# Dilated attention in a hybrid decoder layer: a step takes four heads in the first group and eight in the other two

## The chip, the core and the metric

The kernel runs on one core of a Trainium2 chip. The core has a matrix engine (PE in the profile; its weight loads are a row of their own, PEld), a vector engine (DVE), a scalar engine (ACT), GpSimd (POOL) and SyncE (SP), which here issues most of the loads. Each engine works through its own list of instructions in order and waits for the others at semaphores. The metric is the device time of one launch in microseconds (us); lower is better.

## The reference, cut to what matters

One decoder layer over 512 tokens of 1024 features: an input projection, two token mixers side by side (retention, and a dilated attention), a gated merge, an MLP and a last gated residual. The part that matters here is the dilated attention: 24 heads of 64 features in three groups of eight, with dilations 1, 4 and 16.

```python
DIL_GROUPS = ((128, 1), (512, 4), (2048, 16))      # (window, dilation)
s  = einsum('bcnqhe,bcnkhe->bcnhqk', qs, kk) * hd ** -0.5     # scores, per head
s  = where(mask, s, -1e30)
lse = logsumexp(s, axis=-1)
pr  = exp(s - lse[..., None])
o   = einsum('bcnhqk,bcnkhe->bcnqhe', pr, vv)
...
w = softmax(stack(lses), axis=0)                   # the three groups are merged by their denominators
out = sum(w[..., None] * stack(outs), axis=0)
```

With 512 tokens, each group has four blocks of 128 queries. In group 0 a block sees its own 128 keys and, from the second block on, the 128 before them, so its scores are 128 columns wide in the first block and 256 in the other three. In groups 1 and 2 a block sees 128 keys.

## The kernel before

The layer is one long program of matmuls on PE. Large projections (`gemm`, line 239) keep PE busy; every fp32 operand of theirs is split into a high and a low part (`split`, line 71: ACT writes the high part, DVE the difference), and a product is three matmuls (`PASSES`). The weights come in through SP as tiles of 512 KB (`load_next`, line 94), are split into one of five `w` tiles (`prep_next`, line 109) and are consumed by the matmuls of line 234, each with 512 columns, 24 for one output tile of 128 rows in a projection of depth 1024.

The dilated attention runs inside this stream. `attention` (line 453) makes a list of steps, and `filler` (line 215) hands that list to `pump` (line 205), which is called after every third matmul of a projection and takes out steps at a rate that spreads the whole list over 84 such calls. A unit of attention is one block of 128 queries with `n` heads, and it has three steps:

- `scores` (line 468): one matmul per head (line 475) on 64 partitions of the query and key tiles, the even head on partitions 0 to 63 and the odd one on 64 to 127, into two PSUM banks, `sb[0]` for even heads and `sb[1]` for odd ones. Then DVE adds the mask and takes the row maximum (line 479, per head), scales the maxima (line 482, once), and ACT takes the exponential (line 484, per head, through the helper at line 66).
- `flip` (line 487): PE transposes the exponentials, one 128x128 block at a time (line 493), into a PSUM bank, and ACT copies the bank to SBUF (line 495).
- `weigh` (line 497): two rows of PE work per block of 128 keys and head, with 64 columns each (line 505), sum the values into a bank that belongs to the block of queries; the bank is copied out when all eight heads are in it (line 510).

The steps of three units are staggered: weigh of unit i-2, flip of unit i-1, scores of unit i. A unit has two heads in group 0 and four in groups 1 and 2, so the lists are 48, 24 and 24 steps long.

What stands in which order on an engine is decided by a scheduler when the program is built; the list of steps gives it the program order, and it moves an instruction back when its inputs or its buffer would not be there in time. So transposes and score matmuls of neighbouring steps may end up mixed on PE.

Two pools of SBUF tiles matter: `t` (`big`, 4 KB per partition, 25 tiles), which also holds the weight tiles on their way in, and `s` (`half`, 2 KB, 12 tiles). The PSUM pool of `bank` has four banks.

Of the kernel before, what the change touches and what calls it, by code (L numbers as in the profile page):

```python
# [16 lines left out]
S, D, P = 512, 1024, 128  # L17
# [7 lines left out]
MAGIC = 12582912.0  # L25
TWO_PI = (6.25, 17 / 512, -37 / 2 ** 21, 2 * math.pi - (6.25 + 17 / 512 - 37 / 2 ** 21))
PI_IN = 3.1415925
N_RAW, N_W, N_T, N_S = 4, 5, 25, 12


@with_exitstack
def hybrid_block(ctx, tc, a, out):
    nc = tc.nc
# [12 lines left out]
    def nm(s):  # L46
        count[0] += 1
        return f"{s}{count[0]}"

    def big(shape=(P, D), dtype=F32):  # L50
        return pt.tile(list(shape), dtype, name=nm("t"), tag="t")

    def half(shape=(P, 512), dtype=F32):
        return psm.tile(list(shape), dtype, name=nm("s"), tag="s")

    def stat(n=1):
        return pst.tile([P, n], F32, name=nm("st"), tag=f"st{n}")

    def bank():
        return pps.tile([P, 512], F32, name=nm("b"), tag="ps")  # L60
# [4 lines left out]
    def act(o, i, f=AF.Copy, **kw):  # L65
        nc.scalar.activation(o, i, f, **kw)  # L66
# [39 lines left out]
    def new_w():  # L106
        return pw.tile([P, 2, 2, 512], F32R, name=nm("w"), tag="w")
# [161 lines left out]
    ident = const.tile([P, P], F32, name="ident")  # L269
# [58 lines left out]
    for i in range(4):  # L328
        w = new_w()
        r = pop()  # L330
        for j in range(2):
            f = 2 * i + j
            g = cols[:, 0, f:f + 1]
# [54 lines left out]
    def pair_tiles():  # L388
        return [big((P, 2, 512)) for _ in range(2)]

    def at(pair, i):
        return pair[i // 2][:, i % 2, :]
# [60 lines left out]
    def attention(g, qT, kT, v):  # L453
        n_g = pair_tiles()
        N.append(n_g)
        pairs = 1 if g == 0 else 2
        pvs = {}

        def unit(t, p0):
            nb = 2 if g == 0 and t > 0 else 1  # L460
            w = nb * P
            k0 = (t - nb + 1) * P
            s0, n = 2 * p0, 2 * pairs
            mk = masks[:, 2 - nb:2, :].rearrange("p a b -> p (a b)") if g == 0 else masks[:, g, :]
            mv, dv = M[g][:, t, s0:s0 + n], DEN[g][:, t, s0:s0 + n]
            got = {}

            def scores():
                sb = [bank(), bank()]
                sm = got["p"] = half((P, n, w))  # L470
                st = stat(4)
                for i in range(n):
                    q, hh = divmod(i, 2)
                    rows = slice(hh * 64, hh * 64 + 64)
                    nc.tensor.matmul(sb[hh][:, q * w:(q + 1) * w], at(qT, p0 + q)[rows, t * P:(t + 1) * P],  # L475
                                     at(kT, p0 + q)[rows, k0:k0 + w], start=True, stop=True)
                for i in range(n):
                    q, hh = divmod(i, 2)
                    nc.vector.tensor_tensor_reduce(  # L479
                        out=sm[:, i, :], in0=sb[hh][:, q * w:(q + 1) * w], in1=mk, scale=1.0, scalar=NEG,  # L480
                        op0=OP.add, op1=OP.max, accum_out=mv[:, i:i + 1])
                nc.vector.tensor_scalar(st[:, :n], mv, -0.125, None, op0=OP.mult)  # L482
                for i in range(n):
                    act(sm[:, i, :], sm[:, i, :], AF.Exp, bias=st[:, i:i + 1], scale=0.125,
                        accum_out=dv[:, i:i + 1])

            def flip():
                sm = got["p"]
                tb = bank()
                for i in range(n):  # L490
                    for j in range(nb):
                        c = i * nb + j
                        nc.tensor.transpose(tb[:, c * P:(c + 1) * P], sm[:, i, j * P:(j + 1) * P], ident)  # L493
                pT = got["t"] = half()
                act(pT[:, :n * w], tb[:, :n * w])

            def weigh():
                if t not in pvs:
                    pvs[t] = [bank(), 0]
                pv = pvs[t][0]  # L500
                for i in range(n):
                    s = s0 + i
                    for j in range(nb):
                        c = i * nb + j
                        nc.tensor.matmul(pv[:, s * HD:(s + 1) * HD], got["t"][:, c * P:(c + 1) * P],  # L505
                                         at(v, t - nb + 1 + j)[:, s * HD:(s + 1) * HD],
                                         start=(j == 0), stop=(j == nb - 1))
                pvs[t][1] += n
                if pvs[t][1] == NS:
                    nc.vector.tensor_copy(at(n_g, t), pv)  # L510

            return scores, flip, weigh

        us = [unit(t, p0) for t in range(NT) for p0 in range(0, 4, pairs)]
        steps = []
        for i in range(len(us) + 2):
            for lag in (2, 1, 0):
                if 0 <= i - lag < len(us):
                    steps.append(us[i - lag][lag])
        return steps  # L520
# [7 lines left out]
    for g in range(NG):  # L528
        vs, qT, kT = pair_tiles(), pair_tiles(), pair_tiles()
        gemm(4, uT, plain_evac(vs), k_outer=(g == 0))  # L530
        if g == 0:
            nc.vector.tensor_copy(posr, posr_i)
            rotary(0)

            def tables():
                row_tables()
                scale_rotary(0)
            later(4, tables)
            vc = vs
        else:  # L540
            vc = pair_tiles()
            stream_order(lambda c: at(vc, c), lambda t: at(vs, t))
        gemm(4, uT, rope_evac(qT, g > 0), wstat=True)
        gemm(4, uT, rope_evac(kT, g > 0), wstat=True)
        if g == 0:
            rotary(1)
            scale_rotary(1)
        filler(attention(g, qT, kT, vc), 84, 10)
        if g == 1:
            stream_order(lambda c: sc[0][:, c], lambda t: M[0][:, t])  # L550
            stream_order(lambda c: sc[1][:, c], lambda t: DEN[0][:, t])
# [349 lines left out]
    pT = []  # L901
# [207 lines left out]
    for t in range(NT):  # L1109
        parts_n = 1 if t < NT - 1 else 2  # L1110
        w = 512 // parts_n
# [88 lines left out]
```

## Time and profile before

| | |
|---|---|
| median of 3 runs | 1226.34 us (1225.99 to 1228.89) |
| profiled execution | 1226.16 us, of which the profile's span is 1224.3 us |
| PE busy | 1210.2 us (99%), 5646 matmul rows |
| DVE, ACT, POOL busy | 803.5 us (66%), 595.0 us (49%), 61.5 us (5%) |
| DMA | 158.86 MB, mean 130 GB/s |
| chain that ended last | PE 94%; of it line 234 52%, line 475 2%, line 505 2%, line 493 1% |

PE is busy in nearly every slice of the span. That does not say that it streams at full rate: the profile counts a matmul as busy from its start to its modelled end, and neighbours overlap, so what a piece of PE work costs is read from the starts of the rows around it. A score matmul of line 475 and a weighing matmul of line 505 stand as two rows each in the trace, a transpose of line 493 and a matmul of line 234 as one.

### The profile page before, as it was taken

The page shows a single profiled execution, that of the slowest core. Times are in us where ns is not written, and L with a number is a line of the kernel's source. Part 1 is how long each engine was busy: PE and PEld are TensorE (multiplying, and loading weights), DVE is VectorE, ACT ScalarE, POOL GpSimd, SP SyncE. Part 2 cuts the span into 40 slices and gives each one's busy share as a digit, 9 for nine tenths or more (in the row PEclk, how much of TensorE's full clock was granted, in tenths as well). Part 3 has the DMA queues.
Part 4 walks back from the last instruction along what each step waited for, and adds up shares of the span by engine and source line. Part 5 has one row for each costly group of instructions (what it writes and reads, how often), then busy time and mean ns, then how long its engine had stood idle before and what let it go on. Part 6 is the DMA issues. An engine that isn't in the chain of part 4 may idle for free.

```text
span 1224.3 us, 15136 instructions
## 1 busy us (share of the span) xinstructions
PE 1210.2 (99%) x5646; PEld 990.9 (81%) x5646; DVE 803.5 (66%) x1215; ACT 595.0 (49%) x991; POOL 61.5 (5%) x112
## 2 busy tenths in 40 slices
PE   9999999999999999999999999999999999999996
PEld 7877777887788888888888888887888888888885
DVE  6743643563366895968859555773585776875696
ACT  7344444437765563544535642355544553543362
POOL 1002001000000000000000011020000000000210
PEclk9999999999999999999999999999999999999998
DMA  9422132262105354232435454827132341255401
GB/s 338 152 104 71 60 95 88 69 214 88 44 22 194 137 181 155 85 114 96 145 121 185 134 209 143 297 82 275 52 129 77 121 175 66 86 172 172 155 18 69
DMA packets 53321, 158.86 MB, mean 130 GB/s; under 512 B 8832, under 2 KB 9088, under 8 KB 53248
## 3 DMA queue, kind: packets, MB, share of 16 engines
q1 hardware_dynamic: 39552, 131.82, 30.9%
q10 hardware_dynamic: 9600, 14.53, 3.7%
q0 software_dynamic: 4096, 11.55, 2.6%
q8 instruction: 44, 0.72, 0.2%
q14 instruction: 29, 0.24, 0.1%
HBM read 139.47 MB, written 14.68 MB: 126 GB/s over the span
## 4 chain that ended last, share of the span: by engine, by line
PE 94%; DVE 2%; DMA 1%; ACT 1%; issue 1%; POOL 0%; SPq 0%; DVEq 0%; POOLq 0%; ACTq 0%
PE a L234 52%; PE b L705 15%; PE a L1029 11%; PE a L705 7%; PE b L475 2%; PE b L792 2%; PE b L505 2%; PE b L493 1%; PE b L777 1%; DMA t<-in_w_in_dram 1%; DVE t L294 1%; PE b L813 1%; DVE w L69 0%; DVE s L69 0%; DVE t L69 0%
## 5 line engine op out<-in xcount | busy, mean ns | idle before, releaser
L69 DVE TENSOR_TENSOR w<-t,w 128x1024 fp32r<-128x1024 f32 (+1 forms) x248 | 296.0, 1202 | 152.8 <-ACT w L66 148.4
L66 ACT ACTIVATE w<-t 128x1024 fp32r<-128x1024 f32 (+1 forms) x248 | 257.7, 1045 | 266.5 <-PE a L234 91.3
L234 PE MATMUL a<-u,w 128*128 128x512 f32 x1536 | 374.5, 397 | 0.0
L234 PEld LDWEIGHTS a<-u,w 128*128 128x128 f32 x1536 | 282.3, 188 | 62.1 <-issue 4.0
L69 DVE TENSOR_TENSOR t<-t,t 128x1024 f32<-128x1024 f32 (+4 forms) x179 | 184.8, 1056 | 21.0 <-ACT t L66 18.9
L705 PE MATMUL b<-w,t 128*128 128x512 f32 x696 | 162.5, 389 | 0.0
L705 PEld LDWEIGHTS b<-w,t 128*128 128x128 f32 x696 | 130.6, 188 | 27.1
L1029 PE MATMUL a<-u,w 128*128 128x512 f32 x576 | 134.0, 389 | 0.0
L1029 PEld LDWEIGHTS a<-u,w 128*128 128x128 f32 x576 | 108.1, 188 | 22.5
L234 PE MATMUL a<-w,u 128*128 128x512 f32 (+1 forms) x504 | 116.7, 385 | 1.2 <-ACT w L66 1.0
L234 PE MATMUL a<-t,w 128*128 128x512 f32 x480 | 110.5, 390 | 0.0
L234 PEld LDWEIGHTS a<-w,u 128*128 128x128 f32 x504 | 90.2, 189 | 19.5 <-ACT w L66 1.4
L234 PEld LDWEIGHTS a<-t,w 128*128 128x128 f32 x480 | 89.7, 188 | 18.9 <-DVE t L69 0.3
L234 PE MATMUL a<-w,t 128*128 128x512 f32 x432 | 99.7, 390 | 0.0
L234 PEld LDWEIGHTS a<-w,t 128*128 128x128 f32 x432 | 80.7, 188 | 16.7
L69 DVE TENSOR_TENSOR t<-a,t 128x512 f32<-128x512 f32 x72 | 55.5, 773 | 54.6 <-ACT t L66 31.3
L66 ACT ACTIVATE s<-b 128x512 f32<-128x512 f32 (+1 forms) x74 | 44.7, 606 | 88.7 <-PE b L493 36.0
L479 DVE CUSTOM_DVE_ANT_0 s<-b,masks 128x128 f32<-128x128 f32 (+1 forms) x96 | 27.2, 319 | 83.3 <-PE b L475 83.2
L66 ACT ACTIVATE t<-t 128x512 fp32r<-128x512 f32 (+1 forms) x55 | 42.1, 788 | 38.6 <-DVE t L69 38.5
L66 ACT ACTIVATE s<-s,st 128x128 f32<-128x128 f32 (+1 forms) x96 | 40.0, 418 | 26.5 <-DVE st L482 26.4
L66 ACT ACTIVATE t<-s 128x256 f32<-128x256 f32 (+3 forms) x94 | 41.7, 488 | 22.1 <-DVE s L69 20.3
L66 ACT ACTIVATE s<-a 128x512 f32<-128x512 f32 x56 | 32.7, 593 | 38.7 <-PE a L234 30.3
(119 smaller groups left out, 1018.7 us busy)
## 6 DMA issues: line engine op xcount, KB each, us to landing
t<-in_w_in_dram SPq DMA_DIRECT2D x104, 512.0 KB
t<-in_w_down_dram SPq DMA_DIRECT2D x38, 512.0 KB
t<-in_w_up_dram SPq DMA_DIRECT2D x32, 512.0 KB
t<-in_w_ret_out_dram SPq DMA_DIRECT2D x16, 512.0 KB
t<-in_x_dram SPq DMA_DIRECT2D x8, 512.0 KB
yrd<-s ACTq DMA_DIRECT2D x16, 256.0 KB
t<-yrd SPq DMA_DIRECT2D x16, 256.0 KB
t<-in_w_o_dram SPq DMA_DIRECT2D x8, 512.0 KB
```

Of the source, the lines that this page charges most:

```text
L66: nc.scalar.activation(o, i, f, **kw)
L69: nc.vector.tensor_tensor(o, x, y, op=op)
L234: nc.tensor.matmul(ps, l, r, start=(k == 0 and q == 0), stop=(k == n - 1 and q == 2))
L294: return nc.vector.scalar_tensor_tensor(o, x, s, y, op0=op0, op1=op1)
L475: nc.tensor.matmul(sb[hh][:, q * w:(q + 1) * w], at(qT, p0 + q)[rows, t * P:(t + 1) * P], at(kT, p0 + q)[rows, k0:k0 + w], start=True, sto ...
L479: nc.vector.tensor_tensor_reduce(out=sm[:, i, :], in0=sb[hh][:, q * w:(q + 1) * w], in1=mk, scale=1.0, scalar=NEG, op0=OP.add, op1=OP.max, ...
L493: nc.tensor.transpose(tb[:, c * P:(c + 1) * P], sm[:, i, j * P:(j + 1) * P], ident)
L505: nc.tensor.matmul(pv[:, s * HD:(s + 1) * HD], got["t"][:, c * P:(c + 1) * P], at(v, t - nb + 1 + j)[:, s * HD:(s + 1) * HD], start=(j == ...
L705: nc.tensor.matmul(ps[t], f(k, i, t), w[:, j, k2], start=(first and k == 0 and n == 0), stop=(k == 3 and n == 2), skip_group_check=not first)
L777: nc.tensor.matmul(b[:, :w], kT[d][:, i1, j * P:(j + 1) * P], qT[d][:, i2, j * P:], start=(n == 0), stop=(n == 5))
L792: nc.tensor.matmul(b, sc[j][:, i1, c:c + P], vh[j][:, i2, :], start=(n == 0), stop=(n == last))
L1029: nc.tensor.matmul(state["ps"][t], w[:, i, k2, t * P:(t + 1) * P], vT[:, x, k], start=(k == 0 and n == 0), stop=(k == 7 and n == 2))
```

## The change

`pairs`, the number of head pairs in a unit, goes from 1 to 2 in group 0 and from 2 to 4 in groups 1 and 2. A unit then has four or eight heads, and the lists of steps are 24, 12 and 12 long. What a unit needs grows with it: the score tile and the transposed tile become `big` tiles, the vector of scaled maxima has eight columns, and `flip` fills two banks one after the other, with a copy behind each. The pools go to 26 `t` tiles and 10 `s` tiles. Nothing else is edited; line numbers behind line 497 move by one, the transposes to line 495, their copies to 496 and the weighing matmuls to 506.

```diff
-N_RAW, N_W, N_T, N_S = 4, 5, 25, 12
+N_RAW, N_W, N_T, N_S = 4, 5, 26, 10
...
-        pairs = 1 if g == 0 else 2
+        pairs = 2 if g == 0 else 4
...
                 sb = [bank(), bank()]
-                sm = got["p"] = half((P, n, w))
-                st = stat(4)
+                sm = got["p"] = big((P, n, w))
+                st = stat(8)
...
             def flip():
                 sm = got["p"]
-                tb = bank()
-                for i in range(n):
-                    for j in range(nb):
-                        c = i * nb + j
-                        nc.tensor.transpose(tb[:, c * P:(c + 1) * P], sm[:, i, j * P:(j + 1) * P], ident)
-                pT = got["t"] = half()
-                act(pT[:, :n * w], tb[:, :n * w])
+                pT = got["t"] = big((P, n * w))
+                for h0 in range(0, n * w, 512):
+                    tb = bank()
+                    m = min(512, n * w - h0)
+                    for c in range(h0 // P, (h0 + m) // P):
+                        i, j = divmod(c, nb)
+                        nc.tensor.transpose(tb[:, c * P - h0:(c + 1) * P - h0], sm[:, i, j * P:(j + 1) * P], ident)
+                    act(pT[:, h0:h0 + m], tb[:, :m])
```

The built programs differ in their order from the first score matmul to the end of the attention; ahead of it and behind it the engines' instructions stand in the same order. Three places on PE follow. In the rows, `a` is an accumulator of a projection, `b` a bank, and a row ends with the size of what it writes and with how often it is repeated.

Group 0, last block of queries, before: the scores of a unit (line 475, 256 columns) between the transposes (line 493) of the unit ahead of it.

```order
L234 MATMUL a_1273<-u_134,w_1154 128x512 x3
L493 MATMUL b_1263<-ident,s_1236 128x128 x2
L475 MATMUL b_1280<-t_254,t_252 128x256
L493 MATMUL b_1263<-ident,s_1236 128x128 x2
L475 MATMUL b_1281<-t_254,t_252 128x256
L234 MATMUL a_1273<-u_134,w_1154 128x512 x3
```

The same block of queries now: four heads, with the two even ones and the two odd ones in a stretch each.

```order
L234 MATMUL a_1229<-u_134,w_883 128x512 x6
L475 MATMUL b_1236<-t_254,t_252 128x256 x2
L234 MATMUL a_1229<-u_134,w_1103 128x512 x5
L475 MATMUL b_1237<-t_254,t_252 128x256 x2
L234 MATMUL a_1229<-u_134,w_1103 128x512
```

The transposes have left this place, and two heads on the same partitions follow each other.

Group 2, last block of queries, before: four heads (line 475), each on its own between transposes.

```order
L234 MATMUL a_2686<-u_134,w_2577 128x512 x2
L493 MATMUL b_2671<-ident,s_2616 128x128
L475 MATMUL b_2693<-t_1518,t_1516 128x128
L493 MATMUL b_2671<-ident,s_2616 128x128
L475 MATMUL b_2694<-t_1518,t_1516 128x128
L493 MATMUL b_2671<-ident,s_2616 128x128
L475 MATMUL b_2693<-t_1518,t_1516 128x128
L493 MATMUL b_2671<-ident,s_2616 128x128
L475 MATMUL b_2694<-t_1518,t_1516 128x128
L234 MATMUL a_2686<-u_134,w_2577 128x512 x4
```

The same block now: all eight heads in one stretch, even and odd in turn.

```order
L234 MATMUL a_2587<-u_134,w_2307 128x512 x5
L475 MATMUL b_2594<-t_1466,t_1464 128x128
L475 MATMUL b_2595<-t_1466,t_1464 128x128
L475 MATMUL b_2594<-t_1466,t_1464 128x128
L475 MATMUL b_2595<-t_1466,t_1464 128x128
L475 MATMUL b_2594<-t_1467,t_1465 128x128
L475 MATMUL b_2595<-t_1467,t_1465 128x128
L475 MATMUL b_2594<-t_1467,t_1465 128x128
L475 MATMUL b_2595<-t_1467,t_1465 128x128
L234 MATMUL a_2587<-u_134,w_2491 128x512 x6
```

Four stretches of one head have become one of eight.

Group 1, first block of queries, before: the four heads of the first unit, and the first transpose of that unit behind 17 matmuls of the projection.

```order
L475 MATMUL b_1567<-t_708,t_706 128x128
L475 MATMUL b_1568<-t_708,t_706 128x128
L475 MATMUL b_1567<-t_708,t_706 128x128
L475 MATMUL b_1568<-t_708,t_706 128x128
L234 MATMUL a_1548<-w_1453,u_134 128x512 x6
L234 MATMUL a_1591<-w_1199,u_134 128x512 x6
L234 MATMUL a_1591<-w_1420,u_134 128x512 x5
L493 MATMUL b_1598<-ident,s_1569 128x128
```

The same place now: the second four of eight heads, and the first transposes (line 495) behind 19 matmuls.

```order
L475 MATMUL b_1529<-t_709,t_707 128x128
L475 MATMUL b_1530<-t_709,t_707 128x128
L475 MATMUL b_1529<-t_709,t_707 128x128
L475 MATMUL b_1530<-t_709,t_707 128x128
L234 MATMUL a_1522<-w_1362,u_134 128x512 x4
L234 MATMUL a_1522<-w_1386,u_134 128x512 x6
L234 MATMUL a_1522<-w_1397,u_134 128x512 x6
L234 MATMUL a_1577<-w_1166,u_134 128x512 x3
L495 MATMUL b_1582<-ident,t_1531 128x128 x4
```

Between the scores and the transposes DVE and ACT now have eight heads to treat in place of four, and PE has nearly as much other work there as before.

## Rows read from the trace of the kernel before

**Rows 1.** Head of the profile's page, and its row of the projections' weight loads.

```profile
span 1224.3 us, 15136 instructions
L234 PEld LDWEIGHTS a<-u,w 128*128 128x128 f32 x1536 | 282.3, 188 | 62.1 <-issue 4.0
```

**Rows 2.** Windows: the attention stretch; stretch, length, busy us of each engine (instructions), clock.

```profile
81.73:350.37 268.64, 268.05 (x1378) 209.66 (x1378) 129.14 (x320) 138.79 (x312) 17.27 (x32) 1.00 0.26 83
```

**Rows 3.** Chain of waits, behind the attention stretch; start us, length us, what.

```profile
...
349.90 0.67 PE b L505 x6
...
373.12 0.44 PE b L588 x4
...
384.83 35.38 PE a L234 x156
```

**Rows 4.** Timeline of PE, group 0, first token tile; start us, length us, what.

```profile
89.85 0.86 PE L234 MATMUL a<-w,u 128*128 128x512 f32 x3
90.64 0.49 PE L475 MATMUL b<-t,t 64*128 64x128 f32 x4
91.06 1.66 PE L234 MATMUL a<-w,u 128*128 128x512 f32 x6
92.56 0.22 PE L505 MATMUL b<-t,s 128*128 128x64 f32 x1
```

**Rows 5.** Timeline of PE, group 1.

```profile
211.68 1.54 PE L234 MATMUL a<-u,w 128*128 128x512 f32 x6
213.15 0.71 PE L475 MATMUL b<-t,t 64*128 64x128 f32 x8
213.80 3.02 PE L234 MATMUL a<-u,w 128*128 128x512 f32 x12
216.66 0.33 PE L505 MATMUL b<-t,s 128*128 128x64 f32 x2
```

**Rows 6.** Timeline of PE, group 0, a later token tile (256 columns).

```profile
117.73 0.40 PE L234 MATMUL a<-u,w 128*128 128x512 f32 x1
118.06 0.70 PE L475 MATMUL b<-t,t 64*128 64x256 f32 x4
118.69 1.64 PE L234 MATMUL a<-u,w 128*128 128x512 f32 x6
120.17 0.44 PE L505 MATMUL b<-t,s 128*128 128x64 f32 x3
```

**Rows 7.** Timeline of PE, group 0, scores and transposes mixed.

```profile
130.58 1.32 PE L234 MATMUL a<-u,w 128*128 128x512 f32 x5
131.74 0.38 PE L493 MATMUL b<-ident,s 128*128 128x128 f32 x2
132.05 0.70 PE L475 MATMUL b<-t,t 64*128 64x256 f32 x2
...
133.67 0.96 PE L234 MATMUL a<-u,w 128*128 128x512 f32 x3
134.47 0.33 PE L505 MATMUL b<-t,s 128*128 128x64 f32 x2
```

**Rows 8.** Timeline of PE, group 2, scores and transposes mixed.

```profile
327.44 1.98 PE L234 MATMUL a<-u,w 128*128 128x512 f32 x8
...
331.89 2.56 PE L234 MATMUL a<-u,w 128*128 128x512 f32 x10
334.30 0.33 PE L505 MATMUL b<-t,s 128*128 128x64 f32 x2
```

**Rows 9.** Groups by form: busy us, mean ns of one, idle before and releaser.

```profile
L66 ACT ACT_TABLE_LOAD x25 | 32.1, 1283 | 5.9 <-DMA t<-t 2.8 <-ACT s L66 1.6 <-PEq L1189 1.2
...
L66 ACT ACTIVATE s<-s,st 128x128 f32<-128x128 f32 x72 | 28.1, 391 | 18.4 <-DVE st L482 18.3
...
L479 DVE CUSTOM_DVE_ANT_0 s<-b,masks 128x128 f32<-128x128 f32 x72 | 17.5, 285 | 60.4 <-PE b L475 60.4
```

**Rows 10.** The page's row of the weights' first copies, with ScalarE's idle time before them.

```profile
L66 ACT ACTIVATE w<-t 128x1024 fp32r<-128x1024 f32 (+1 forms) x248 | 257.7, 1045 | 266.5 <-PE a L234 91.3
```

## The prediction

> **What bounds the kernel now.** I read the views from the outside in. The head of the page gives a span of 1224.3 us [rows 1]; the profiled execution took 1226.16 us, and the sum below is made against that. The windows of the attention stretch, from the first score matmul to the last weighing one, show PE busy for 268.05 of 268.64 us at the full granted clock, 2.4 GHz, while DVE is busy for 129 and ACT for 139 [rows 2]. So only what PE itself does, or is made to wait for, counts here. The chain of waits gives PE's undisturbed rates behind the stretch: 156 projection matmuls in 35.38 us, 0.227 us each; four transposes in 0.44 us, 0.11 each; six weighing rows in 0.67 us, 0.112 each [rows 3].
>
> With these rates the stretch can be taken apart. Of its 1378 PE rows [rows 2], 96 heads of two rows are scores, 120 transposes and 240 weighing rows, which leaves 826 projection matmuls: 826 x 0.227 = 187.5 us, 120 x 0.11 = 13.2, 240 x 0.112 = 26.9. The scores are left with 268.6 - 227.6 = 41.0 us, 0.43 us a head, though a head's matmul writes only 128 or 256 columns. The timeline of PE shows why. I price a stretch of scores from the start of a projection row ahead of it to the start of the row behind the next projection matmuls, less 0.227 for each of those:
>
> - two heads of 128 columns: 92.56 - 89.85 = 2.71, less nine matmuls: 0.67 us [rows 4];
> - four heads of 128 columns: 216.66 - 211.68 = 4.98, less 18 matmuls: 0.89 us [rows 5].
>
> Two further heads add 0.22, so a head costs 0.11 and a stretch, whatever its length, 0.45: what PE pays to go over to matmuls on 64 partitions and back. Two heads of 256 columns: 120.17 - 117.73 = 2.44, less seven matmuls, 0.85 [rows 6], so 0.20 a head beside the 0.45. Where transposes stand between the scores, every piece pays again: two single heads of 256 columns between four transposes take 134.47 - 130.58 = 3.89, less eight matmuls (1.82) and four transposes (0.44): 1.63, or 0.82 a piece [rows 7]; four single heads of 128 columns take 334.30 - 327.44 = 6.86, less 18 matmuls (4.09) and four transposes (0.44): 2.33, or 0.58 a piece [rows 8].
>
> **The change part by part.** *Scores on PE.* Their matmuls are the same 96; what changes is into how many stretches the order cuts them. In the order before there are 52: of 128 columns fifteen with one head, five with two, one with three, eleven with four; of 256 columns sixteen with one, four with two. In the order after there are 24: of 128 columns two with one, one with two, five with four, six with eight; of 256 columns two with one, two with three, two with four, and four in which two heads on the same partitions follow each other.
>
> Before: 15 x 0.58 + 5 x 0.67 + 0.89 (three heads priced as four) + 11 x 0.89 = 22.7, and 16 x 0.82 + 4 x 0.85 = 16.5; together 39.2 us. The 1.8 us to the 41.0 left above are short waits and other seams.
>
> After: eight heads of 128 columns are not in the trace. Bounds: one stretch of four, 0.89, below, and two such stretches, 1.78, above; I take 0.45 + 8 x 0.11 = 1.33, since the rows with two and four heads differ by just this slope. Four of 256 columns likewise: 0.45 + 4 x 0.20 = 1.25 (between 0.85 and 1.70), three the same 1.25. Two heads on the same partitions can't run side by side: between a pair, 0.85, and two single pieces, 1.63, I take the middle, 1.24. Sum: 2 x 0.58 + 0.67 + 5 x 0.89 + 6 x 1.33 = 14.3, and 2 x 0.82 + 2 x 1.25 + 2 x 1.25 + 4 x 1.24 = 11.6; together 25.9 us. Saved: 39.2 - 25.9 = 13.3 us.
>
> *Transposes and weighing.* Their counts stay 120 and 120. They run on all 128 partitions like the projections, and a transpose costs the same 0.11 alone or in eights as far as rows 3 tell, so I cost the grouping at nothing.
>
> *DVE and ACT.* Sixteen scalings of maxima and two bank copies go, and the order has 15 table loads of ACT where the trace shows 25, at 1.28 us each [rows 9]. All this is covered by PE, which pauses for 0.6 us in the whole stretch [rows 2]; it is worth nothing on the path, and if a wait for ACT should appear these 12.8 us only help.
>
> *Longer steps.* In a unit the work of DVE and ACT between scores and transposes doubles. A reduction keeps DVE busy for 17.5/72 = 0.24 us and an exponential ACT for 28.1/72 = 0.39 [rows 9], so eight heads need 8 x 0.24 + 8 x 0.39 = 5.0 us until the last exponential, but the first transpose needs only the first: 1.9 + 0.4 = 2.3. In the order PE has 19 projection matmuls (4.3 us) between them in the first unit of group 1, 20 in that of group 2, and about 50 (11.4 us) in the others of these groups. There each transpose of the second bank comes one matmul after the other, 0.34 us apart, about the pace of the exponentials. I cost the waits at nothing here and carry them as a rival.
>
> *Tiles.* Scores and transposed scores now live in the pool that also takes the weight loads, which grows by one tile. ACT's first copy of a weight tile waits, by its releaser, for PE to free a split tile, not for a load [rows 10], so loads are early, and I cost this at nothing.
>
> The sum: 1226.16 - 13.3 = 1212.9 us. The median of the runs shown is 0.18 above the profiled execution, hence 1213.0.
>
> **The rivals.** *The exponentials come late.* Eight heads need 5.0 us and the shortest distance is 4.3: 0.7 us short at the two first units, more if ACT has weight copies of 1.05 us [rows 10] in between. If each of the 16 units lost 0.45 us, 7.2 in all, the time would be 1220.2. For it speaks that one more bank than the pool of four is asked for in a step; against it, that 14 units have more room, and that PE lost only 0.6 us of the whole stretch before [rows 2], where 17 matmuls lay at the place of these 19.
>
> *Only pairing pays.* If a stretch had no price of its own and just a head without a partner on the other 64 partitions were dear, the gain would be that of the pairs alone: a single head costs 0.82 - 0.65 = 0.17 more at 256 columns and 0.58 - 0.56 = 0.02 at 128, so 16 x 0.17 + 15 x 0.02 = 3.0 before, and 12 x 0.17 + 2 x 0.02 = 2.1 after; 0.9 us saved, 1225.3. Against it: rows 4 and 5 are both fully paired, and the second pair costs a third of the first. A rule of the Trainium skill leads to this rival: "TensorE: Matmul & The Clock Gate", Part 3 on packing small matmuls, says that a weight load overlaps with running matmuls only when its row group differs. By it every projection matmul would show its load, and going over to the scores would cost nothing special. The trace disagrees: loads of 0.188 us [rows 1] on the same 128 rows lie behind each other's matmuls at 0.227 a step [rows 3].
>
> *Weights come late, and the kernel is slower.* Up to two score tiles and two transposed ones now hold `t` tiles, three more than the pool grew by, and a weight load must wait until PE has weighed a unit before it finds a tile. Place: the split of the next projection's weights, and PE's line 234 behind it. The stretch holds 826/96 = 8.6 projections; the gain is eaten from 13.3/8.6 = 1.5 us of wait in each, and at 2.1 us the time is 1231. Against it stands rows 10: ACT waits there for PE.
>
> **How the numbers follow.** The forecast's own range: if the unexplained 1.8 us go too, and the same-partition pairs cost 0.85, 13.3 + 1.8 + 1.6 = 16.7 are saved, 1209.6 by the median; rounding of 52 prices by 0.02 adds 1.0, hence 1208.6. If eight heads cost 1.78 and those pairs 1.63, 13.3 - 2.7 - 1.6 = 9.0, hence 1217.3. Late exponentials reach to 1220.2, and I let the range end there. Chances: forecast 0.82, late exponentials 0.10, only pairing 0.03, late weights 0.03, and 0.02 for more gain than the range holds. A measurement of this kernel tells about 0.3%, 3.7 us, from no change. Faster by more than that: 0.82 + 0.09 + 0.02 = 0.93; within it: 0.01 of the late exponentials and only pairing, 0.04; slower: 0.03.
>
> **What would show it.** In the timeline after, a stretch of eight score heads (16 rows of line 475) should cost 1.33 us by the same reckoning; 1.78 or more says that the price goes with the heads. The stretch of attention should be some 13 us shorter for nearly the same number of projection matmuls, with PE busy throughout. Waits of PE at line 495 for ACT would show late exponentials, waits of line 234 for ACT or DVE with a DMA ahead late weights. The prediction is wrong if the attention stretch keeps its length, or if the gain is there and lost again behind it.

## The result and the profile after

The changed kernel takes 1212.24 us (median; 1212.09 to 1212.70) beside 1226.26 us for the kernel before in the same session: a ratio of 0.9882, with a 95% interval of 0.9868 to 0.9895. That is 14.0 us less; the prediction was 1213.0 us, 13.3 less than the median it started from.

The head of the page, and three of its groups (columns as in [rows 9]):

```profile
span 1210.6 us, 15131 instructions
...
L66 ACT ACTIVATE w<-t 128x1024 fp32r<-128x1024 f32 (+1 forms) x248 | 256.9, 1044 | 261.9 <-PE a L234 93.7
...
L234 PE MATMUL a<-u,w 128*128 128x512 f32 x1536 | 369.0, 395 | 1.0 <-ACT t L66 1.0
L234 PEld LDWEIGHTS a<-u,w 128*128 128x128 f32 x1536 | 284.0, 188 | 62.1 <-issue 2.3
```

The span is 13.7 us shorter. The weight copies of ScalarE have the same duration and releaser as in [rows 10]. The chain of waits of this trace can be followed back only to 64 us before the end, so the stages are read from the windows: ahead of the first score matmul, from there to the last weighing one, and behind it (columns as in [rows 2]).

```profile
0.00:83.20 83.20, 80.47 (x344) 65.61 (x344) 52.83 (x78) 40.97 (x64) 4.78 (x12) 1.00 0.62 218
83.20:336.25 253.05, 252.83 (x1372) 206.46 (x1371) 129.54 (x318) 129.26 (x306) 17.27 (x32) 1.00 0.27 88
336.25:1210.60 874.35, 863.58 (x3934) 717.25 (x3932) 618.42 (x804) 408.83 (x609) 39.46 (x68) 1.00 0.38 135
```

The attention stretch went from 268.64 us [rows 2] to 253.05, 15.6 less. It starts 1.5 us later and holds six PE rows fewer (1372, not 1378): six projection matmuls, 1.4 us, now stand ahead of it. The rest, 14.2 us, is gained inside the stretch; what lies behind is 0.4 us longer (873.93 us before). The granted clock is full in all three.

By the prediction's reckoning, 820 projection matmuls take 186.1 us, 120 transposes 13.2 and 240 weighing rows 26.9, so that the scores are left with 26.8 us, where they had 41.0.

Timeline of PE, group 2: a stretch of eight heads (start us, length us, what).

```profile
312.82 3.57 PE L234 MATMUL a<-u,w 128*128 128x512 f32 x15
316.32 1.16 PE L475 MATMUL b<-t,t 64*128 64x128 f32 x16
317.41 5.06 PE L234 MATMUL a<-u,w 128*128 128x512 f32 x21
322.31 1.89 PE L506 MATMUL b<-t,t 128*128 128x64 f32 x16
```

322.31 - 312.82 = 9.49, less 36 projection matmuls (8.17): 1.32 us for eight heads, where four cost 0.89 [rows 5].

The same view in group 0: twice two heads of 256 columns on the same 64 partitions. At two other places of this group the even and odd heads of a unit stand together, eight rows of 256 columns; one of them comes second.

```profile
144.60 1.29 PE L234 MATMUL a<-u,w 128*128 128x512 f32 x5
145.82 1.13 PE L475 MATMUL b<-t,t 64*128 64x256 f32 x4
146.88 1.43 PE L234 MATMUL a<-u,w 128*128 128x512 f32 x5
148.24 1.13 PE L475 MATMUL b<-t,t 64*128 64x256 f32 x4
149.30 1.19 PE L234 MATMUL a<-u,w 128*128 128x512 f32 x4
150.32 0.33 PE L506 MATMUL b<-t,t 128*128 128x64 f32 x2
```

```profile
99.91 1.13 PE L475 MATMUL b<-t,t 64*128 64x256 f32 x8
100.97 2.33 PE L234 MATMUL a<-u,w 128*128 128x512 f32 x9
```

The first gives (150.32 - 144.60 - 14 x 0.227) / 2 = 1.27 us for two heads. From the first score row to the next projection row it is 1.06 us in both fences: four heads in pairs cost what two heads on one half cost.

What going over to 64 partitions does is seen most directly in the waits of the weight loads (engine, line, what ended the wait: us in total, times, longest), before and then after, in the attention stretch.

```profile
PEld b L475 <- issue: 10.0, 38, 0.4
PEld a L234 <- issue: 4.0, 12, 0.3
PEld b L493 <- ACT s L66: 2.2, 5, 1.0
```

```profile
PEld b L475 <- issue: 6.3, 20, 0.4
PEld a L234 <- issue: 2.3, 7, 0.3
PEld b L495 <- ACT t L66: 0.9, 3, 0.3
```

"Issue" means that nothing in the profile ended the wait: the load of the first score of a stretch stood still though its inputs were there, 38 times before and 20 times after, for 0.26 and 0.32 us on average. The second line is the way back, the first load of a projection behind the scores: 12 times and 7. The last line is where late exponentials would stand: 0.9 us after, less than the 2.2 us before.

ScalarE and VectorE, the lines that answer to [rows 9]:

```profile
L66 ACT ACTIVATE t<-t,st 128x128 f32<-128x128 f32 x72 | 27.9, 390 | 14.5 <-DVE st L482 14.5
L66 ACT ACT_TABLE_LOAD x15 | 19.2, 1283 | 4.0 <-DMA t<-t 1.9 <-PEq L1190 1.2 <-ACT s L66 0.8
...
L479 DVE CUSTOM_DVE_ANT_0 t<-b,masks 128x128 f32<-128x128 f32 x72 | 16.2, 285 | 16.7 <-PE b L475 16.7
```

The ten table loads did go.

### The profile page after: what moved, and what is told of

Its sections match the earlier page's. It is cut to its first block, busy times and chain, and to the rows that moved or that the text cites. A ratio compares the mean times of both kernels' runs of the same rounds, so it can differ in the third digit from the quotient of the medians.

```text
span 1210.6 us, 15131 instructions
## 1 busy us (share of the span) xinstructions
PE 1196.9 (99%) x5646; PEld 989.3 (82%) x5646; DVE 800.8 (66%) x1199; ACT 579.1 (48%) x979; POOL 61.5 (5%) x112
## 5 line engine op out<-in xcount | busy, mean ns | idle before, releaser
L234 PE MATMUL a<-u,w 128*128 128x512 f32 x1536 | 369.0, 395 | 1.0 <-ACT t L66 1.0
L1030 PE MATMUL a<-u,w 128*128 128x512 f32 x576 | 134.0, 390 | 0.0
L66 ACT ACTIVATE t<-a 80x512 f32<-80x512 f32 (+1 forms) x32 | 18.9, 591 | 69.6 <-PE a L234 64.8
L69 DVE TENSOR_TENSOR s<-a,t 128x512 f32<-128x512 f32 x40 | 26.4, 687 | 37.1 <-PE a L234 30.2
L66 ACT ACTIVATE t<-t,st 128x128 f32<-128x128 f32 (+1 forms) x96 | 39.8, 416 | 22.5 <-DVE st L482 19.4
```

The lines of the kernel that those rows point to most:

```text
L69: nc.vector.tensor_tensor(o, x, y, op=op)
L234: nc.tensor.matmul(ps, l, r, start=(k == 0 and q == 0), stop=(k == n - 1 and q == 2))
L1030: nc.tensor.matmul(state["ps"][t], w[:, i, k2, t * P:(t + 1) * P], vT[:, x, k], start=(k == 0 and n == 0), stop=(k == 7 and n == 2))
```

## The experiments

The theory: the gain is that of 28 stretches of scores fewer, each of which costs PE about 0.45 us to go over to matmuls on 64 partitions and back. Its rivals: the pools or the fewer, larger steps of VectorE and ScalarE bring it; one group alone brings it; or it comes from heads that find a partner on the other 64 partitions. Times are medians, beside the kernel before on the same chip: 1226.41 us for the first four, 1226.88 for the other four. "Scores" is the reckoning above, from the window of each run's own attention stretch.

**The pools alone.** The kernel before with the pools of the change:

```diff
-N_RAW, N_W, N_T, N_S = 4, 5, 25, 12
+N_RAW, N_W, N_T, N_S = 4, 5, 26, 10
```

> The kernel before with the tile pools of the change alone (26 t tiles and 10 s tiles); units and steps as before, 52 stretches of score matmuls in the order. Theory (a stretch of scores on 64 partitions has a price of its own, about 0.45 us, and the change pays by having fewer of them): no difference, 1226 us. Rival (the pools give the gain): 1212 us. Rival (ten s tiles cost something that the change hides): above 1230 us.

Measured: 1227.03 us, ratio 1.0003 (0.9994 to 1.0013). The pools by themselves are worth nothing.

**Group 0 alone, groups 1 and 2 alone.** The changed kernel with the larger step in one part of the groups:

```diff
-        pairs = 2 if g == 0 else 4
+        pairs = 2 if g == 0 else 2
```

> The change in group 0 alone (four heads a unit there, four in the others as before). The order has 38 stretches of scores. Theory, by the prices of the prediction: of 128 columns 11 x 0.58 + 3 x 0.67 + 14 x 0.89 = 20.9, of 256 columns 11.6, together 32.5 us against 39.2 before: 6.7 saved, 1219.5 us. Rival (every step saved is worth the same, 13.9 us over 48 steps): 24 steps saved, 1219.3 us; the two theories are told apart by the other runs.

```diff
-        pairs = 2 if g == 0 else 4
+        pairs = 1 if g == 0 else 4
```

> The change in groups 1 and 2 alone (eight heads a unit there, two in group 0 as before). The order has 37 stretches of scores. Theory, by the prices of the prediction: of 128 columns 2 x 0.58 + 3 x 0.67 + 4 x 0.89 + 6 x 1.33 = 14.7, of 256 columns 20 x 0.82 + 2 x 0.85 = 18.1, together 32.8 us against 39.2: 6.4 saved, 1219.9 us. Rival (every step saved is worth the same): 24 steps saved, 1219.3 us. With the run of group 0 alone: if the two gains add up to that of the whole change, the groups don't help or hinder each other.

Measured: 1219.40 us (0.9941, 0.9927 to 0.9956) and 1219.59 us (0.9944, 0.9929 to 0.9958), gains of 7.0 and 6.8 us. Their sum, 13.8, is the whole change's 14.0: the parts add up, as prices per stretch do, and neither group's gain hides behind the other's. A price per step, 14.0 us over 48 steps, would give 7.0 us for each of the two as well; these runs don't tell the two apart, the next one does.

**The small units in another order.** The kernel before, with all its 96 steps, its pools and its copies, but weigh, scores, flip in a round in place of weigh, flip, scores, so that the scores of a unit no longer come right behind the transposes of the unit ahead:

```diff
-            for lag in (2, 1, 0):
+            for lag in (2, 0, 1):
```

> The kernel before, its small units and all 96 steps; only the three steps of an iteration are listed in another order (weigh, scores, flip in place of weigh, flip, scores). The order on PE then has 32 stretches of scores, all of them paired and none mixed with transposes: 4 x 0.67 + 16 x 0.89 + 12 x 0.85 = 27.1 us against 39.2. Theory (the price is of the stretches): 12.1 saved, 1214 us, with not one step fewer. Rival (what counts is the number of steps or the size of a unit): no difference, 1226 us.

Measured: 1215.87 us, ratio 0.9912 (0.9895 to 0.9928). The window of its attention stretch, and a wait in PE's timeline:

```profile
83.00:339.50 256.50, 255.91 (x1378) 203.85 (x1377) 133.05 (x334) 133.23 (x310) 17.32 (x32) 1.00 0.27 87
```

```profile
185.25 0.84 PE L234 MATMUL a<-w,u 128*128 128x512 f32 x3
186.64 0.72 PE L475 MATMUL b<-t,t 64*128 64x128 f32 x8 [0.55 <-DVE t L69]
```

With no step fewer, three quarters of the gain are there: 10.5 of 14.0 us. So it isn't the number of steps, of scalings of maxima or of copies that counts. What changed is that 52 stretches became 32, and that every head now stands beside a partner on the other 64 partitions, where before 32 heads didn't; the next three runs part these two. Scores are 256.50 - 227.6 = 28.9 us, where the prices of [rows 4 to 6] give 4 x 0.67 + 16 x 0.89 + 12 x 0.85 = 27.1. Of the 1.8 us between them, 0.55 is the wait above, for the keys that VectorE writes; the rest was not followed up. The kernel before had 1.8 us of such a rest too (41.0 beside 39.2), so in the stretch itself the expected 12.1 us are all there (268.64 to 256.50). The profiled execution lost part of them outside it: its stretch starts 1.3 us later, and what lies behind takes 1.0 us longer (1214.40 - 339.50 = 874.90 us, beside 873.93). Why was not tried.

**The same matmuls on all partitions, in both kernels.** Each score matmul takes all 128 partitions, so PE never goes over to 64. These two kernels leave out the separation of a pair's heads: what a head's matmul sums is both of them.

```diff
-                    rows = slice(hh * 64, hh * 64 + 64)
+                    rows = slice(0, P)
```

> The kernel before, with the score matmuls on all 128 partitions in place of 64, in exactly the same places of the order (52 stretches, mixed with transposes as before). It leaves out the separation of a pair's heads: each score is the sum of the two, so its numbers are not the reference's. Theory (the price of a stretch is that of going over to matmuls on 64 partitions and back): the 0.45 us of 52 stretches go, and heads no longer run side by side, so they cost about 0.22 us at 128 columns and 0.43 at 256: 72 x 0.22 + 24 x 0.43 = 26.2 us against 39.2, 13.0 saved, 1213 us. Rival (mixing short matmuls with others is dear by itself, whatever partitions they use): the stretches keep their price and the lost pairing comes on top, 72 x 0.11 + 24 x 0.2 = 12.7 us less what single heads paid already, 3: 1236 us.

> The changed kernel with the score matmuls on all 128 partitions, in the same places (24 stretches). As in the run before, each score is the sum of a pair's two heads. Theory: stretches cost nothing of their own here, so this and the kernel before with all partitions should take about the same, 26.2 us of scores and 1213 us, though one has 52 and the other 24 stretches; against the changed kernel nearly nothing changes (its scores cost 25.9 by the same prices). Rival (the number of stretches or of steps counts by itself): the two differ by 13 us as the kernels with 64 partitions do.

Measured: 1215.55 us with the order before (0.9908, 0.9894 to 0.9923), 1214.35 us with the order after (0.9894, 0.9878 to 0.9911). Their windows:

```profile
82.31:339.66 257.35, 256.74 (x1378) 216.89 (x1376) 129.40 (x320) 138.55 (x312) 17.32 (x32) 1.00 0.27 87
```

```profile
84.50:338.98 254.48, 254.28 (x1372) 217.12 (x1370) 129.90 (x318) 129.33 (x306) 17.32 (x32) 1.00 0.27 88
```

Where nothing goes over to 64 partitions, 52 stretches and 24 differ by 1.2 us, not by 14. The waits of weight loads for "issue" at line 475 are gone; what is left of waits of loads in the stretch of the second of the two is this:

```profile
PEld b L475 <- DVE t L69: 0.5, 1, 0.5
PEld b L495 <- ACT t L66: 0.2, 1, 0.2
```

And at a place where transposes stand between the scores, in the first of the two:

```profile
110.25 1.42 PE L234 MATMUL a<-u,w 128*128 128x512 f32 x5
111.50 0.38 PE L493 MATMUL b<-ident,s 128*128 128x128 f32 x2
111.72 0.60 PE L475 MATMUL b<-t,t 128*128 128x256 f32 x2
112.15 0.38 PE L493 MATMUL b<-ident,s 128*128 128x128 f32 x2
112.37 0.60 PE L475 MATMUL b<-t,t 128*128 128x256 f32 x2
112.62 0.82 PE L234 MATMUL a<-u,w 128*128 128x512 f32 x2
113.27 0.27 PE L505 MATMUL b<-t,s 128*128 128x64 f32 x1
```

113.27 - 110.25 = 3.02, less seven projection matmuls (1.59) and four transposes (0.44): 0.99, or 0.50 a piece, of which the head's own rows are 0.43 (112.15 - 111.72). The same mixture cost 0.82 a piece [rows 7] with heads on 64 partitions. Both runs came out 1.4 to 2.6 us later than expected, with scores of 29.8 and 28.3 us: a stretch has a small price, here 0.07, even without going over. By the difference of the two runs it is less, 1.2 us over 28 stretches, 0.04 each; that is rough, since the four times of the second run alone spread over 2.3 us.

**No pairs, but 64 partitions.** The changed kernel with every head on partitions 0 to 63; half of the heads then use the other's data, so the kernel leaves out their scores.

```diff
-                    rows = slice(hh * 64, hh * 64 + 64)
+                    rows = slice(0, 64)
```

> The changed kernel with all heads on partitions 0 to 63, in the same places of the order: the odd head of a pair is computed from the even one's features, so the numbers are not the reference's. It takes the pairing away and keeps 24 stretches on 64 partitions. Theory: only the pairing is lost, 0.11 us for each of some 70 heads of 128 columns and 0.2 for the 12 heads of 256 columns that had a partner, 10 us in all: 1222 us. Rival (only pairing pays, stretches are free): the gain of the change was pairing, so it goes and more: 1226 us or above.

Measured: 1223.23 us, ratio to before 0.9967 (0.9956 to 0.9978). The window, and then a stretch of four heads and one of eight (8 and 16 rows), first in the timeline of this run and then in that of the run with the order after on all partitions:

```profile
84.84:347.91 263.07, 263.07 (x1372) 216.26 (x1371) 129.84 (x318) 129.31 (x306) 17.32 (x32) 1.00 0.26 85
```

```profile
189.80 1.16 PE L475 MATMUL b<-t,t 64*128 64x128 f32 x8
190.89 0.74 PE L234 MATMUL a<-w,u 128*128 128x512 f32 x2
...
327.12 2.05 PE L475 MATMUL b<-t,t 64*128 64x128 f32 x16
329.10 5.06 PE L234 MATMUL a<-u,w 128*128 128x512 f32 x21
```

```profile
184.29 1.05 PE L475 MATMUL b<-t,t 128*128 128x128 f32 x8
185.09 0.71 PE L234 MATMUL a<-w,u 128*128 128x512 f32 x2
...
318.48 1.95 PE L475 MATMUL b<-t,t 128*128 128x128 f32 x16
320.18 4.11 PE L234 MATMUL a<-u,w 128*128 128x512 f32 x17
```

Two things come out of it. First the worth of pairs: from the first score row to the next projection row, eight heads take 1.98 us on one half and 1.09 on both (317.41 - 316.32 in the first timeline of after); 0.11 a head, and 10 to 11 us over the whole kernel. Pairing is dear to lose, and the change brings some of it: by the counts of the prediction 32 of the 96 heads had no partner before, 16 of each width, and 14 have none after, two of 128 columns and twelve of 256. At 0.11 and 0.20 us a head that is about 2.3 us of the 14.2. It can't be the main thing: this run has no pairs at all, and it is still 3.7 us faster than the kernel before, where 64 heads had a partner.

Second the price of going over, by itself. This run and the one on all partitions have the same order of instructions and no pairs; they differ in the number of partitions. 1223.23 - 1214.35 = 8.9 us over 24 stretches is 0.37 us each. That it goes by the stretch and not by the head, the two lengths show: from the first score row to the next projection row four heads take 1.09 us on one half and 0.80 on all partitions, eight take 1.98 and 1.70. Four further heads add 0.89 and 0.90, 0.22 a head in both, and the difference stays at 0.29 and 0.28; the rest of the 0.37 would lie ahead of the first score row, which this measure leaves out. With the 0.04 to 0.07 of any stretch this makes 0.41 to 0.44, beside the 0.45 taken from [rows 4, 5]. The Trainium skill has a sentence on this ("TensorEngine Tiling (Array Packing)", Tiling Modes, Key Properties): a change of the tiling mode, not of the tile alone, drains TensorE. The trace agrees as to the price: going from one half to the other inside a stretch shows none (by [rows 4, 5] and the eight heads of after, each further head in a stretch of pairs adds 0.11 us), while leaving all 128 partitions and coming back costs 0.37 us. No row shows the drain itself.

**The change in the other order.** If stretches are what counts, the changed kernel still has some to save: 24 can be 17, with none between transposes.

```diff
-            for lag in (2, 1, 0):
+            for lag in (2, 0, 1):
```

> The changed kernel with the steps of an iteration listed as weigh, scores, flip. The order then has 17 stretches of scores, none mixed with transposes and all 256-column ones paired in fours: 0.58 + 2 x 0.89 + 1.22 + 7 x 1.33 = 12.9 and 6 x 1.25 = 7.5, together 20.4 us against 25.9 for the changed kernel: 5.5 saved, 1206.7 us. Rival (what was to be had from longer units is had; the transposes now come closer to their exponentials or further from their banks and PE waits): 1212 us or above.

Measured: 1206.81 us (1206.38 to 1207.65), ratio to before 0.9837 (0.9822 to 0.9852). That is 20.1 us under the kernel before of its session, and 5.4 under the median of the changed one, faster than both (the two ratios to the kernel before, 0.9837 and 0.9882, are from two sessions; their intervals don't meet). The window, and waits of weight loads in it:

```profile
83.94:331.30 247.36, 247.36 (x1372) 204.81 (x1371) 132.10 (x320) 131.54 (x308) 17.32 (x32) 1.00 0.28 92
```

```profile
PEld b L475 <- issue: 5.2, 15, 0.4
...
PEld b L475 <- DVE t L511: 0.7, 2, 0.4
PEld b L506 <- ACT t L66: 0.4, 1, 0.4
```

PE has no idle time in the whole stretch, and the scores are left with 247.36 - 226.2 = 21.1 us.

## Why the prediction was right, step by step

- **What bounds the kernel**: PE's order in the attention stretch. Right: the whole gain lies in that window, and PE is busy for 252.83 of its 253.05 us after.
- **A stretch costs 0.45 us, a head 0.11 or 0.20**: right, and now shown apart: 0.37 us for going over and back, 0.04 to 0.07 for any stretch, and the head's share doubles without its partner, from 0.11 to 0.22 at 128 columns.
- **Eight heads of 128 columns**, taken as 1.33 between 0.89 and 1.78: 1.32. The price of a stretch doesn't grow with its length.
- **Two heads on the same partitions**, taken as 1.24 between 0.85 and 1.63: 1.27. The size was right, but the middle was chosen without a mechanism, and the timeline has one: they are one stretch, not two, and cost what four paired heads do, 1.06 us from the first score row to the next projection row, since heads without a partner lose only the overlap.
- **The sum**: 13.3 us expected of the scores, 14.2 measured (41.0 to 26.8). The prices explained 39.2 before and explain 25.9 now; the part left unexplained fell from 1.8 to 0.9 us. The span is shorter by 14.2 less the 0.4 behind the stretch and 0.1 ahead of it, 13.7; the medians, 14.0 apart, stand 0.8 us under the forecast. PE's idle time in the window fell from 0.59 to 0.22 us, which is part of it; where the rest is, wasn't tried.
- **Costed at nothing**: grouped transposes and weighing, scalings, copies and table loads. Right within what the sum leaves open, though [rows 3] show transposes only four in a row, and not alone or in eights as the prediction has it. That ScalarE's ten table loads, 12.8 us, show nowhere in the time agrees with the cover named for them.
- **Late exponentials** (0.10): didn't come; loads of transposes waited for ScalarE for 0.9 us in all.
- **Only pairing pays** (0.03): fell. A kernel with no pairs at all but 24 stretches is 3.7 us faster than the one before. Pairs have a share, though, and one larger than the 0.9 us that the rival was priced at: about 2.3 us by the prices of the runs, while 28 stretches at 0.37 to 0.45 us are 10.4 to 12.6. The forecast's sum holds this share already, since it prices single heads by what they took.
- **Weights come late** (0.03): didn't come; the waits of the weight copies are as before and the pools alone changed nothing.

## What to carry to other kernels

Where matmuls on 64 partitions stand in a stream of matmuls on 128, count how often PE goes over and back, not how many small matmuls there are; put those of a step together, each beside a partner on the other half, and keep transposes out from between them. The order of the steps is the first thing to try: one line of it gave 10.5 us without larger tiles, and 5.4 more on top of them. To find such a price, take the stream's undisturbed rate from a place without small work, subtract, and compare stretches of different length: the slope is the work, and what is left at no work is the crossing.

## What the runs showed of the hardware

A score matmul on half the partitions next to one on the other half costs half as much as alone: 0.11 us a head of 128 columns in pairs and 0.22 on one half. Taking all 128 partitions costs 0.22 a head too, so alone a head gains nothing by being half as deep, and the crossing comes on top: eight heads take 1.70 us on all partitions (320.18 - 318.48) and 1.98 on one half. For single heads of 256 columns between transposes it is 0.50 us a piece on all partitions and 0.82 on 64. So a kernel that can't bring its small matmuls together, or can't pair them, gains nothing by making them small and pays the crossing. The runs on all 128 partitions sum both heads of a pair; what it would cost to get each head's own scores that way was not tried.
